# Attention with probabilities left unnormalised, and the reciprocal sums applied to the output

## The chip, the cores and the metric

The kernel runs on one core of one Trainium2 chip. The metric is device time in microseconds (us). The kernel before took 1541.53 us, the median of three runs (1538.05 to 1544.7). Its profiled execution took 1538.8 us, with a span of 1536.8 us from the first to the last instruction.

The core has five engines with a queue each: TensorE (PE; its weight loads are listed as PEld), VectorE (DVE), ScalarE (ACT), GpSimd (POOL) and SyncE (SP, which issues loads). TensorE writes PSUM only; VectorE and ScalarE read PSUM.

## The reference

One layer of a streaming encoder over 1024 frames of width 1024. Three token mixers run side by side on a normalised input, are gated and merged, and a feed-forward part follows. Two of the mixers are attention with 4 heads of 64: mixer A looks at a band of nine chunks of 64 frames with a relative bias, mixer B at the 256 keys that an indexer selects. Cut to what the change touches:

```
sc = q . k * d ** -0.5 + bias            # A: banded, B: masked to the selected keys
p  = softmax(sc)                         # exp(sc - max) / sum, over the keys
o  = p @ v                               # one 64-wide output per head and frame
...
merged = sigmoid(gt) * (y @ w_branch)    # summed over the three mixers
x = x + merged @ w_out
x = x + (silu(g) * u) @ w_ffn_out
```

Dividing the probabilities by their sum before the product with v, or the product by the sum after it, gives the same output.

## The kernel before, in words

Frames lie in 8 tiles of 128. All weights are split into a high and a low part (ScalarE copies, VectorE subtracts), and most products are three matmuls (`mm3`, L118 to L121) in that form. Streams of work are written as generators: A and B (attention), C (the recurrent mixer), G, F and W (gates), Z, Y (projections), K (top-k of the indexer, 32 counting rounds on VectorE and ScalarE), T. The string ORDER (L39) says which stream takes its next step. That is the order of the program. The order on each engine is then made by a planner that runs a timeline of its own (`schedule_with_timeline_sim=True`, L1461), so steps of neighbouring streams are interleaved, instruction by instruction. Each engine executes its queue in that order.

`attention` (L390) does one tile of 128 frames for two heads of mixer A or B. It is called for 8 tiles, two pairs of heads and two mixers: 32 calls, 64 heads. For each head, the scores go to PSUM (`dots`, L237). VectorE adds the mask or bias and takes the minimum of the negated scores into `nm` (L400). ScalarE takes the exponential of the row and its sum (L403). VectorE takes the reciprocal of the sum (L405) and multiplies the row with it (L406). TensorE transposes the row in blocks of 128 keys (L412) into banks of the pool tag T, which has two banks, and ScalarE copies them to SBUF as PT (L413). When both heads are done, the output `o` takes a bank of T too; per block of keys, one matmul for each head (L420) adds to its 64 rows of `o`, and ScalarE copies the result to `yT` (L422). A row has 128 to 640 keys in mixer A and 128 to 1024 in mixer B.

`sl` is a list of SBUF slots of 4 KB per partition; a tile takes the first free one and gives it back at the end of the list. `tbank` (L140) gives a PSUM bank of tag T. The T banks are also used by the turning of queries and keys (L352) and by some gate products.

Of the kernel before, what the change touches and what calls it, by code (L numbers as in the profile page):

```python
# [10 lines left out]
F32 = mybir.dt.float32  # L11
# [3 lines left out]
AF = mybir.ActivationFunctionType  # L15
OP = mybir.AluOpType
# [64 lines left out]
def hybrid_kernel(ctx: ExitStack, tc: tile.TileContext, x, small, cs, bias_a, lru_w, w_idx, w_zg, w_c, w_g, w_b,  # L81
                  w_o, w_fi, w_fo, out):
    nc = tc.nc
    V, S, G, PE = nc.vector, nc.scalar, nc.gpsimd, nc.tensor
    const = ctx.enter_context(tc.tile_pool(name="const", bufs=1))
    arena = ctx.enter_context(tc.tile_pool(name="arena", bufs=1))
    dram = ctx.enter_context(tc.tile_pool(name="dram", bufs=1, space=bass.MemoryType.DRAM))
    sl = Slots(arena, range(NRING, NSLOT))
    ring = Slots(arena, range(NRING))

    ident = const.tile([128, 128], F32, name="ident")
# [42 lines left out]
    def gbank(shape=(128, 512)):  # L134
        return psum.tile(list(shape), F32, name="G", tag="G", bufs=2)

    def sbank(shape=(128, 1024)):
        return psum.tile(list(shape), F32, name="S", tag="S", bufs=2)

    def tbank(shape=(128, 512)):  # L140
        return psum.tile(list(shape), F32, name="T", tag="T", bufs=2)
# [29 lines left out]
    for t0, tn in BATCH:  # L171
# [8 lines left out]
        w = 128 * tn  # L180
        for k in range(KD):
            if k % 2 == 0:
                sb = sbank()
            p = sb[:, 512 * (k % 2):512 * (k % 2) + w]
# [45 lines left out]
    def dots(sb, q, kh, kl, k0, w):  # L230
        o = 128 if w == 640 else 0
        segs = [(0, min(512 - o, max(w, 256)))]
        if w > 512 - o:
            segs.append((512 - o, w))
        for c0, c1 in segs:
            PE.matmul(sb[:, o + c0:o + c1], lhsT=q, rhs=kh[:, k0 + c0:k0 + c1], start=True, stop=False)
            PE.matmul(sb[:, o + c0:o + c1], lhsT=q, rhs=kl[:, k0 + c0:k0 + c1], start=False, stop=True)  # L237
        return sb[:, o:o + w]
# [4 lines left out]
    for g in range(2):  # L243
        zq = sl.get((128, 4, 4, 64), F32, "zq")
        zk = sl.get((128, 4, 2, 64), F32, "zk")
        for j in range(4):
            t = 4 * g + j
            p = gbank((128, 324))
# [49 lines left out]
    for i in range(2, NT):  # L298
        w = (i + 1) * 128
# [90 lines left out]
    def attention(i, b0, pr, qk, v, mask, yT, isB=False):  # L390
        nb = i + 1 - b0
        w = nb * 128
        q, kh, kl = qk
        PT = []
        for e in range(2):
            h = 2 * pr + e
            sb = dots(sbank(), q[e][:, 128 * i:128 * i + 128], kh[e], kl[e], 128 * b0, w)
            P = sl.get((128, 1024), F32, "P")
            nm = const.tile([128, 1], F32, name="nm", bufs=4)
            V.tensor_tensor_reduce(P[:, 0:w], sb, mask(h), -1.0, 3.0e38, op0=OP.add,  # L400
                                   op1=OP.min, accum_out=nm)
            sm_ = const.tile([128, 1], F32, name="sum", bufs=4)
            S.activation(P[:, 0:w], P[:, 0:w], AF.Exp, bias=nm, scale=-1.0, accum_out=sm_)  # L403
            rc = const.tile([128, 1], F32, name="rc", bufs=4)
            V.reciprocal(rc, sm_)  # L405
            V.tensor_scalar(P[:, 0:w], P[:, 0:w], rc, None, op0=OP.mult)  # L406
            pt_s = sl.get((128, 8, 128), F32, "PT")
            for c0 in range(0, nb, 4):
                c1 = min(c0 + 4, nb)
                pt = tbank((128, 4, 128))  # L410
                for b in range(c0, c1):
                    PE.transpose(pt[:, b - c0], P[:, 128 * b:128 * b + 128], ident)  # L412
                S.activation(pt_s[:, c0:c1], pt[:, 0:c1 - c0], AF.Copy)  # L413
            sl.free(P)
            PT.append(pt_s)
        o = tbank((128, 128))
        for b in range(nb):
            for e in range(2):
                h = 2 * pr + e
                PE.matmul(o[64 * e:64 * e + 64, :], lhsT=v[(b0 + b) // 4][:, (b0 + b) % 4, h, :],  # L420
                          rhs=PT[e][:, b, :], start=b == 0, stop=b == nb - 1, skip_group_check=True)
        S.activation(yT[:, 128 * i:128 * i + 128], o, AF.Copy)  # L422
        sl.free(*PT)

    def steps_A():
        for pr in range(2):
            bA = []
            for h in (2 * pr, 2 * pr + 1):
                bt = sl.get((128, 640), F32, "biasA")
                nc.gpsimd.dma_start(bt, bias_a[h])  # L430
                bA.append(bt)
            yA = sl.get((128, T), F32, "yA")
            qk = to_stack(zA[pr], ga8, smc("ga", 1))
            for i in range(NT):
                b0 = max(0, i - 4)
                w = (i + 1 - b0) * 128
                attention(i, b0, pr, qk, vA, lambda h: bA[h % 2][:, 640 - w:640], yA)
                if i == NT - 1:
                    sl.free(*bA)
                    nc.gpsimd.dma_start(y_dram[pr], yA)  # L440
                    sl.free(yA)
                    for a in qk:
                        sl.free(*a)
                    if pr == 1:
                        sl.free(*vA)
                yield
# [287 lines left out]
    def steps_B():  # L734
        for pr in range(2):
            yB = sl.get((128, T), F32, "yB")
            qk = to_stack(zB[pr], None, None)
            for i in range(NT):
                w = (i + 1) * 128
                mk = mask[i] if i >= 2 else m01[:, 256 - w:256]  # L740
                attention(i, 0, pr, qk, vB, lambda h: mk, yB, True)
                if i == NT - 1:
                    nc.gpsimd.dma_start(y_dram[2 + pr], yB)
                    sl.free(yB)
                    for a in qk:
                        sl.free(*a)
                    if pr == 1:
                        sl.free(*vB, *mp)
                yield
# [50 lines left out]
    def mbank():  # L800
        nb_[0] += 1
        return (gbank, tbank, sbank)[nb_[0] // 2 % 3]()[:, 0:512]
# [106 lines left out]
    yT = {}  # L909
# [34 lines left out]
    for ot in range(8):  # L944
# [13 lines left out]
        for q, (b, ks) in enumerate(((2, (4, 5, 6, 7)), (0, (0, 1)), (1, (2, 3)))):  # L958
            gt = load_gate(3 * ot + b) if ot else g0[b]
            mt = sl.get((128, T), F32, "mt") if q else None  # L960
            for hf in range(2):
                c = slice(512 * hf, 512 * hf + 512)
                m = M[ot // 2][hf][:, ot % 2]
                p = mbank()
# [107 lines left out]
    def bank(shape=(128, 512), at=0):  # L1072
        return psum.tile(list(shape), F32, name="B", tag=f"B{at}")

    for s_, n in enumerate(order):
# [5 lines left out]
        for t in range(4):  # L1081
            if n in "167":
                p = X[t]
            else:
                p = bank(at=4 + t)
# [379 lines left out]
```

## Time and profile before

| | before |
|---|---|
| median of three runs | 1541.53 us |
| profiled execution | 1538.8 us |
| its span | 1536.8 us |
| PE busy | 1479.5 us (96%) |
| PEld busy | 1237.1 us (80%) |
| DVE busy | 1119.4 us (73%) |
| ACT busy | 760.7 us (49%) |
| POOL busy | 108.4 us (7%) |
| mean granted TensorE clock | 0.991 |

The rows below are from the trace of the profiled execution. Times in timelines are microseconds from the start of the span. A group of instructions is given by line, engine, operation, output and inputs, shape and count, then after the bar its busy time in us and the mean duration of one in ns, then the idle time of its engine just before it and what ended that idle time. The granted clock is a share of TensorE's full 2.4 GHz. Matmuls overlap each other, so the time that one takes of the engine is read from start to start.

### The profile page before, as it was taken

The numbers are of one execution on the slowest core, as the hardware profiler recorded it, in microseconds if no ns is written. First come the engines' busy times: TensorE is split into PE (matmuls) and PEld (weight loads), VectorE is DVE, ScalarE is ACT, GpSimd is POOL, SyncE is SP. The second block draws the span as 40 slices with busy tenths as digits, with TensorE's granted clock in tenths as the row PEclk, the third lists the DMA queues.
The fourth block names the chain that finished last, engine by engine and source line by source line (L and its number), as shares of the span: only waits on it lengthen the run. The fifth ranks groups of instructions, "written<-read, shape, count | busy, mean of one in ns | idle before, by whom it ended". The sixth has DMA issues, their size and how long they took to land.

```text
span 1536.8 us, 19968 instructions
## 1 busy us (share of the span) xinstructions
PE 1479.5 (96%) x7612; PEld 1237.1 (80%) x7612; DVE 1119.4 (73%) x1949; ACT 760.7 (49%) x1188; POOL 108.4 (7%) x162
## 2 busy tenths in 40 slices
PE   6999889999999998999998989999999999999998
PEld 5898788989778886788886868888888888788887
DVE  4789999869666779767889786555555556478872
ACT  5566768774768656443214463333333333354340
POOL 1120011210000110010000210000000000000000
PEclk9999999999999999999999999999999999999999
DMA  4011202112112022357552322323232323697532
GB/s 175 28 45 42 96 18 97 56 69 83 41 42 69 29 96 70 117 178 300 213 182 79 110 96 96 110 96 110 96 110 96 110 96 123 231 364 267 189 126 89
DMA packets 51088, 178.40 MB, mean 116 GB/s; under 512 B 5872, under 2 KB 6000, under 8 KB 50992
## 3 DMA queue, kind: packets, MB, share of 16 engines
q1 hardware_dynamic: 36576, 128.36, 24.4%
q0 software_dynamic: 12688, 45.62, 7.6%
q10 hardware_dynamic: 1728, 3.15, 0.5%
q8 instruction: 60, 0.98, 0.3%
q14 instruction: 36, 0.29, 0.1%
HBM read 131.75 MB, written 45.35 MB: 115 GB/s over the span
## 4 chain that ended last, share of the span: by engine, by line
PE 63%; DVE 7%; ACT 3%; DMA 2%; issue 1%; SPq 0%; DVEq 0%; ACTq 0%
PE B L120 14%; PE B L121 14%; PE B L119 14%; PE G L121 4%; PE G L119 4%; PE G L120 4%; PE T L120 1%; PE T L119 1%; PE T L121 1%; PE S L119 1%; DMA fa<-pd 1%; PE S L121 1%; PE S L120 1%; PE T L420 1%; DVE ol L104 1%
## 5 line engine op out<-in xcount | busy, mean ns | idle before, releaser
L120 PE MATMUL B<-hl,fwh 128*128 128x512 f32 x528 | 205.5, 391 | 3.2 <-DVE hl L104 3.2
L119 PE MATMUL B<-hh,fwh 128*128 128x512 f32 x528 | 202.5, 391 | 3.3 <-ACT hh L103 3.3
L121 PE MATMUL B<-hh,fwl 128*128 128x512 f32 x528 | 198.3, 391 | 0.0
L119 PEld LDWEIGHTS B<-hh,fwh 128*128 128x128 f32 x528 | 99.5, 188 | 25.0 <-ACT hh L103 4.2
L120 PEld LDWEIGHTS B<-hl,fwh 128*128 128x128 f32 x528 | 99.5, 188 | 24.8 <-DVE hl L104 4.3
L121 PEld LDWEIGHTS B<-hh,fwl 128*128 128x128 f32 x528 | 99.6, 189 | 20.7
L120 PE MATMUL G<-wzl,hTh 128*128 128x256 f32 x384 | 110.9, 289 | 3.1 <-DVE wzl L104 3.1
L119 PE MATMUL G<-wzh,hTh 128*128 128x256 f32 x384 | 110.4, 290 | 1.3 <-ACT wzh L103 0.6
L121 PE MATMUL G<-wzh,hTl 128*128 128x256 f32 x384 | 110.9, 289 | 0.0
L104 DVE TENSOR_TENSOR fwl<-s,fwh 128x1024 fp32r<-128x1024 f32 x44 | 53.9, 1225 | 78.2 <-PE B L120 77.4
L120 PE MATMUL B<-fol,foh 128*128 128x512 f32 x264 | 102.8, 389 | 0.5 <-DVE fol L104 0.5
L119 PE MATMUL B<-foh,foh 128*128 128x512 f32 x264 | 101.4, 390 | 1.8 <-ACT foh L103 1.8
L121 PE MATMUL B<-foh,fol 128*128 128x512 f32 x264 | 101.7, 389 | 0.0
L649 ACT ACTIVATE junk_s<-score,ngS 128x1024 int8<-128x1024 f32 (+2 forms) x78 | 77.5, 993 | 17.3 <-DVE ngS L647 13.1
L121 PE MATMUL G<-hTh,wgl 128*128 128x512 f32 x192 | 76.5, 398 | 2.0 <-DVE wgl L104 2.0
L120 PEld LDWEIGHTS G<-wzl,hTh 128*128 128x128 f32 x384 | 74.5, 194 | 4.6 <-DVE wzl L104 3.7
L119 PE MATMUL G<-hTh,wgh 128*128 128x512 f32 x192 | 76.3, 397 | 1.1 <-ACT ge L544 1.1
L119 PEld LDWEIGHTS G<-wzh,hTh 128*128 128x128 f32 x384 | 74.6, 195 | 3.1 <-ACT wzh L103 1.1
L120 PE MATMUL G<-hTl,wgh 128*128 128x512 f32 x192 | 76.1, 396 | 0.0
L121 PEld LDWEIGHTS G<-wzh,hTl 128*128 128x128 f32 x384 | 74.7, 194 | 0.8 <-issue 0.5
L103 ACT ACTIVATE fw<-fb 128x512 fp32r<-128x512 f32 x22 | 13.9, 634 | 121.7 <-PE B L121 120.7
L103 ACT ACTIVATE foh<-fa 128x1024 fp32r<-128x1024 f32 x33 | 35.0, 1060 | 58.7 <-DMA fa<-pd 38.2
(488 smaller groups left out, 3863.6 us busy)
## 6 DMA issues: line engine op xcount, KB each, us to landing
fw<-in_w_fo SPq DMA_DIRECT2D x33, 512.0 KB, 5.4
fa<-pd SPq DMA_DIRECT2D x33, 512.0 KB, 5.1
gl<-gd SPq DMA_DIRECT2D x24, 512.0 KB, 6.0
fa<-in_w_fi SPq DMA_DIRECT2D x22, 512.0 KB, 3.6
fb<-in_w_fi SPq DMA_DIRECT2D x22, 512.0 KB, 3.5
pd<-act POOLq DMA_DIRECT2D x22, 512.0 KB, 5.3
ga<-in_w_g SPq DMA_DIRECT2D x18, 512.0 KB, 3.6
x<-in_x SPq DMA_DIRECT2D x12, 512.0 KB, 4.4
```

What stands on the lines that cost most here:

```text
L103: S.activation(hi, raw, AF.Copy)
L104: (eng or V).tensor_tensor(lo, raw, hi.bitcast(F32), op=OP.subtract)
L119: PE.matmul(o, lhsT=lh, rhs=rh, start=first, stop=False, **kw)
L120: PE.matmul(o, lhsT=lh, rhs=rl, start=False, stop=False, **kw)
L121: PE.matmul(o, lhsT=ll, rhs=rh, start=False, stop=last, **kw)
L420: PE.matmul(o[64 * e:64 * e + 64, :], lhsT=v[(b0 + b) // 4][:, (b0 + b) % 4, h, :], rhs=PT[e][:, b, :], start=b == 0, stop=b == nb - 1, sk ...
L649: S.activation(junk_s[:, 0:(i + 1) * 128], score[i], AF.Sign, bias=self.ng.bitcast(F32)[:, j:j + 1], accum_out=self.cnt[:, j:j + 1])
```

## The change

The probabilities stay as the exponential gives them. The two sums of a pair of heads go into the two columns of one tile. One reciprocal on VectorE writes each of them to 64 columns, 128 in all. TensorE transposes this 128x128 tile into the second half of the bank that holds the output, and ScalarE copies it to SBUF, into the first columns of the second head's P, which is for that reason given back only at the end of the call. The output matmuls follow. VectorE multiplies the output, read from PSUM, with that copy and writes `yT`, in place of ScalarE's copy. The slots of P of the second head and of both PT are given back in one call, in that order.

```diff
@@ attention
+        sums = const.tile([128, 2], F32, name="sum", bufs=4)
         for e in range(2):
...
-            sm_ = const.tile([128, 1], F32, name="sum", bufs=4)
-            S.activation(P[:, 0:w], P[:, 0:w], AF.Exp, bias=nm, scale=-1.0, accum_out=sm_)
-            rc = const.tile([128, 1], F32, name="rc", bufs=4)
-            V.reciprocal(rc, sm_)
-            V.tensor_scalar(P[:, 0:w], P[:, 0:w], rc, None, op0=OP.mult)
+            S.activation(P[:, 0:w], P[:, 0:w], AF.Exp, bias=nm, scale=-1.0, accum_out=sums[:, e:e + 1])
...
-            sl.free(P)
+            if e == 0:
+                sl.free(P)
             PT.append(pt_s)
-        o = tbank((128, 128))
+
+        rc = const.tile([128, 2, 64], F32, name="rc")
+        V.reciprocal(rc, sums[:, :, None].to_broadcast([128, 2, 64]))
+        on = tbank((128, 256))
+        o, n = on[:, 0:128], on[:, 128:256]
+        PE.transpose(n, rc.rearrange("p h d -> p (h d)"), ident)
+        ns = P[:, 0:128]
+        S.activation(ns, n, AF.Copy)
         for b in range(nb):
...
-        S.activation(yT[:, 128 * i:128 * i + 128], o, AF.Copy)
-        sl.free(*PT)
+        V.tensor_mul(yT[:, 128 * i:128 * i + 128], o, ns)
+        sl.free(P, *PT)
```

## Rows read from the trace of the kernel before

**Rows 1.** The page, part 1: busy us, share of the span, instructions.

```profile
PE 1479.5 (96%) x7612; PEld 1237.1 (80%) x7612; DVE 1119.4 (73%) x1949; ACT 760.7 (49%) x1188; POOL 108.4 (7%) x162
```

**Rows 2.** Stretches: length, PE, PEld, DVE, ACT, POOL busy (count), clock, DMA share, GB/s.

```profile
150.00:175.00 25.00, 21.50 (x109) 16.18 (x107) 24.75 (x91) 18.43 (x39) 0.55 (x1) 1.00 0.19 62
175.00:200.00 25.00, 20.17 (x115) 16.62 (x114) 24.71 (x83) 20.08 (x39) 1.07 (x2) 0.93 0.23 85
200.00:225.00 25.00, 24.20 (x210) 22.70 (x210) 23.27 (x76) 16.25 (x35) 3.73 (x4) 0.93 0.06 15
...
295.00:330.00 35.00, 35.00 (x233) 30.73 (x232) 26.34 (x62) 26.70 (x56) 5.28 (x4) 1.00 0.18 61
...
590.00:610.00 20.00, 17.04 (x164) 13.46 (x165) 19.89 (x29) 13.79 (x29) 0.53 (x1) 1.00 0.15 43
```

**Rows 3.** Waits of PE, 120 to 610 us: who for whom, total us, times, longest.

```profile
PE G L120 <- DVE wzl L104: 3.1, 1, 3.1
PE T L412 <- ACT yA L422: 2.7, 2, 1.7
...
PE T L412 <- ACT PT L413: 1.8, 3, 1.0
...
PE T L420 <- ACT PT L413: 1.1, 4, 0.5
PE T L412 <- DVE P L406: 0.6, 1, 0.6
```

**Rows 4.** Groups of DVE instructions: the multiplication by shapes, and the smallest masked add.

```profile
L406 DVE TENSOR_SCALAR P<-P,rc 128x640 f32<-128x640 f32 (+7 forms) x64 | 31.0, 491 | 0.6
...
L406 DVE TENSOR_SCALAR P<-P,rc 128x640 f32<-128x640 f32 x20 | 11.0, 550 | 0.2
...
L406 DVE TENSOR_SCALAR P<-P,rc 128x512 f32<-128x512 f32 x8 | 3.8, 483 | 0.1
L406 DVE TENSOR_SCALAR P<-P,rc 128x384 f32<-128x384 f32 x8 | 3.3, 414 | 0.1
...
L406 DVE TENSOR_SCALAR P<-P,rc 128x256 f32<-128x256 f32 x8 | 2.7, 349 | 0.1
...
L406 DVE TENSOR_SCALAR P<-P,rc 128x128 f32<-128x128 f32 x8 | 2.2, 290 | 0.1
...
L400 DVE CUSTOM_DVE_ANT_0 P<-S,biasA 128x128 f32<-128x128 f32 x4 | 1.1, 290 | 0.1
```

**Rows 5.** Views of single lines: ns min/median/max, first and last start in us.

```profile
L405 DVE RECIPROCAL rc<-sum x64: 136/157/165, 135.8 to 593.9; 128x1 f32<-128x1 f32 x64
...
L469 DVE RECIPROCAL sp_w<-sp_w x1: 173/173/173, 119.8 to 119.8; 128x4 f32<-128x4 f32 x1
...
L413 ACT ACTIVATE PT<-T x96: 253/490/616, 145.0 to 605.7; 128x512 f32<-128x512 f32 x44, 128x128 f32<-128x128 f32 x28, 128x256 f32<-128x256 f32 x12, 128x384 f32<-128x384 f32 x12
...
L422 ACT ACTIVATE yB<-T x16: 257/277/280, 406.3 to 607.6; 128x128 f32<-128x128 f32 x16
```

**Rows 6.** PE timeline at 208.5 us: start us, us, engine, line, operation.

```profile
208.49 0.28 PE L119 MATMUL G<-wzh,hTh 128*128 128x256 f32 x1
208.61 0.27 PE L412 MATMUL T<-ident,P 128*128 128x128 f32 x1
208.64 0.36 PE L120 MATMUL G<-wzl,hTh 128*128 128x256 f32 x1
208.84 0.28 PE L121 MATMUL G<-wzh,hTl 128*128 128x256 f32 x1
```

**Rows 7.** DVE timeline in the tail, 589 to 602 us.

```profile
590.64 0.16 DVE L405 RECIPROCAL rc<-sum 128x1 f32<-128x1 f32 x1
...
591.45 0.75 DVE L406 TENSOR_SCALAR P<-P,rc 128x1024 f32<-128x1024 f32 x1
...
593.92 0.15 DVE L405 RECIPROCAL rc<-sum 128x1 f32<-128x1 f32 x1
...
598.20 0.75 DVE L406 TENSOR_SCALAR P<-P,rc 128x1024 f32<-128x1024 f32 x1
```

## The prediction

> **What bounds the kernel now.** I read the page's engine shares first. TensorE is busy for 1479.5 of 1536.8 us, VectorE for 1119.4 [rows 1], so over the whole run TensorE sets the time and only its 57 us of idle time can be won. The change touches nothing before the first reciprocal at 135.8 us and nothing after the last output copy at 607.6 us [rows 5]; outside of that window the work stays as it is. So I then read the busy time by stretches inside it, looking for stretches where TensorE is not full, and who is full instead. Between 150 and 225 us VectorE is busy for 24.75 of 25, 24.71 of 25 and 23.27 of 25 us, while TensorE has 3.5, 4.8 and 0.8 us of idle time, and its granted clock in the last two of these stretches is 0.93, so it ran part of each at 1.2 instead of 2.4 GHz [rows 2]. There VectorE is the bound: it runs the top-k counting and the weight splits beside the first pair of local-attention heads. From 295 to 330 us it is the other way round, TensorE full and VectorE at 26.34 of 35 us. In the tail, 590 to 610 us, VectorE is again full (19.89 of 20) and TensorE has 3.0 us idle [rows 2]. The list of TensorE's waits over 120 to 610 us says what it waited for by name: 3.1 us for a weight split on VectorE (wzl), 2.7 us for the copy of an attention output out of PSUM (yA, two times in 32), 1.8 and 1.1 us for copies of transposed probabilities (PT), and only 0.6 us, once, for the multiplication that the change removes (P, L406) [rows 3].
>
> **The change part by part.** One head at one tile is a head-tile, of which there are 64; two heads at one tile make a pair-tile, of which there are 32.
>
> Removed on VectorE. Each head loses a one-column reciprocal of 157 ns [rows 5] and a multiplication of its probabilities. For the first pair of local heads, tiles 0 to 7, the widths are 128, 256, 384, 512 and four times 640: 290 + 349 + 414 + 483 + 4 x 550 = 3736 ns a head [rows 4]. Two heads: 7.5 us, and 16 x 0.157 = 2.5 us, so 10.0 us leave the stage in which VectorE is the bound.
>
> Added on VectorE, per pair-tile: a reciprocal written to 128 columns, and a product of 128x128 with one operand in PSUM. The product is like the smallest masked add, 128x128 out of PSUM, 290 ns [rows 4]. The wide reciprocal is not in the trace. Its rows are one column at 157 ns (136 at the least) and four columns at 173 ns [rows 5]: (173-157)/3 = 5.3 ns per column, so 157 + 127 x 5.3 = 0.83 us. Bounds: if it streamed like the multiplication it replaces, (550-290)/512 = 0.51 ns per column [rows 4], it is 0.22 us; from the fastest one-column reciprocal, (173-136)/3 = 12.3 ns per column, it is 1.70 us. I take 0.83, which comes from the medians. In the first stage that is 8 x (0.83+0.29) = 9.0 us, against 10.0 removed: -1.0 us, with ends 8 x 0.51 - 10.0 = -5.9 and 8 x 1.99 - 10.0 = +5.9. Because VectorE is the bound there, I count it in full. In the other three pairs of heads (24 pair-tiles) I count nothing: they run mostly where VectorE has slack, as in the 295 to 330 us stretch. If that cover were gone, the whole of it, 32 x 1.12 = 35.8 us added against 64 x 0.157 + 31.0 = 41.0 removed [rows 4, 5], would still be in the kernel's favour.
>
> The Trainium skill, "VectorE: DVE Perf Modes", section "First, the fixed hardware budget", says that the reciprocal is an iterative division with a repeat count of 8; with the 0.96 GHz of VectorE from the page "Trainium Kernel Development and Optimization" (NeuronCore Architecture), an estimate is 8.3 ns per column and 0.157 + 127 x 0.0083 = 1.21 us. The row's 5.3 ns per column lies below this and far above one cycle. By that rule the first stage would gain 8 x 1.50 - 10.0 = +2.0 us of VectorE work instead of losing 1.0.
>
> Added on TensorE: 32 transposes of 128x128. A single one among other matmuls stands in the trace, with starts at 208.49 (matmul), 208.61 (transpose), 208.64 and 208.84 (matmuls) [rows 6]. From 208.49 to 208.84 run two matmuls and the transpose, 0.35 us; a matmul alone takes 208.61 - 208.49 = 0.12, two 0.24. So 0.11 us each, 32 x 0.11 = +3.5 us. TensorE is the bound outside of the VectorE-bound stretches and the work comes on top, so this term is nearly sure; its low end is 0 for the 12 pair-tiles that lie in those stretches (8 in the first stage, 4 in the tail), 20 x 0.11 = 2.2.
>
> Added wait of the output matmuls. The transposed reciprocals n and the output o are halves of one tile in one PSUM bank; ScalarE copies n out before o may be written. On TensorE the 2 to 16 output matmuls are queued behind this, and all that follows in its order. The copy is as long as the old output copy, about 0.27 us [rows 5], and ScalarE's total is the same: one copy of 128x128 in, one out. Cover: the order of each engine is planned by a timeline, which puts other streams' matmuls in between. How well that works is seen on the 96 PT copies: 1.8 + 1.1 = 2.9 us of waits [rows 3, 5], 0.03 us each, so 32 x 0.03 = 1.0 us. In the last four pair-tiles there is hardly anything to put in between, and I count the copy as exposed: 4 x 0.27 = 1.1 us. Bounds: 0, and 32 x 0.27 = 8.6 us.
>
> For this wait the Trainium skill has a rule: "PSUM — Partial Sum Buffer", section "Terms", says that two engines at the same bank at once are an error, so the matmuls cannot slip under the copy; without the rule the 2.1 us of this term would be 0. No run shown so far tells which.
>
> Moved: the output leaves PSUM by a VectorE product instead of a ScalarE copy. That frees the bank for the next transposes, one of two banks that they all share. TensorE waited on this copy twice, 2.7 us [rows 3]. On VectorE the product stands in a fuller queue: a reciprocal and the multiplication that follows it with nothing else to wait for lie 0.81 us apart at 590.64 and 4.28 us apart at 593.92 [rows 7]. I add 0.8 us to each of those two waits, +1.6 us; ends 0 and 2 x 4.3 = 8.6.
>
> Removed wait: transposes follow the exponential directly, -0.6 us [rows 3]. What is late next is the copy PT, already in the sum. The second head's P stays allocated until the product; its two PT tiles were and are freed in the same call, so the order of the slots is unchanged and I cost it at nothing; if a later tile did need that slot early, it would wait one product, 0.29 us. No DMA is added or passed.
>
> Sum: 3.5 + 1.0 + 1.1 + 1.6 - 1.0 - 0.6 = +5.6 us. The profiled execution took 1538.8 us (span 1536.8 and 2.0 around it), which gives 1544.4. The median of the three runs, 1541.5, is 2.7 above the profiled one; the forecast for the median is 1547 us. By the reciprocal of the skill's page it would be 3.0 more, 1550.
>
> **Rivals.**
> *Faster: VectorE is relieved.* The reciprocal streams at 0.22 us, the first stage loses 5.9 us, TensorE's waits for splits there go, and with them the two stretches at 0.93 of the clock (2 x 25 x 0.07 = 3.5 us): -5.9 - 3.5 + 3.5 - 0.6 = -6.5, 1535. For it: 9.1 us of TensorE idle time at 150 to 225 us [rows 2]. Against it: the four-column reciprocal.
> *Slower: the reciprocal is the bill.* At 1.70 us the VectorE-bound stage grows by 5.9 instead of shrinking by 1.0: +12.5, 1554. This is also the case in which the change does not do what it says, take work off VectorE; it decides from about 0.96 us per reciprocal, where 8 x (0.96+0.29) = 10.0. For it: the two reciprocal rows; against it: they are single fast calls whose start-up may hide columns.
> *Slower: the bank is held.* If in the 12 pair-tiles where VectorE is full (8 in the first stage, 4 in the tail) each product keeps the bank 0.81 us longer and TensorE has nothing else to issue, 12 x 0.81 = 9.7 in place of 1.6: +13.7, 1555. For it: TensorE's longest attention wait is on just this release; against it: 30 of 32 releases cost nothing before. It decides when the waits on the output's release pass about 5 us.
> Besides, each engine's order is planned anew by the timeline, which can move some us either way; this widens all cases.
>
> **How the numbers follow.** Forecast 0.50, faster rival 0.15, reciprocal 0.18, bank 0.17. About 0.5% (7.7 us) is what a measurement of this kernel can tell from no change; from 1541.5 that is 1533.8 to 1549.2. The faster rival's own 1535 falls just short of it; with a favourable order of the rest it would pass, and so might a few of the forecast's cases: 0.14 faster. The two slower rivals nearly all lie above, and a tail of the forecast: 0.37 slower, 0.49 the same. The forecast's own range is 1541 to 1550; the range that leaves out two in ten is 1534 to 1558, from a little below the faster rival to a little above the slower ones.
>
> **What would show it.** In the profile after: 32 reciprocals of 128 columns near 0.83 us (0.22 or 1.70 would give a rival); no multiplication of P; VectorE busy some 5 us less (35.8 against 41.0); 32 more transposes, TensorE's instruction count up by 32; its waits on the ScalarE copy of n near 2 us, on the output's product near 4 us, on wzl in the 150 to 225 us stretch as before. ScalarE unchanged within 1 us. The prediction is wrong if the attention window ends earlier than before by several us, or if the time moves outside 128 to 610 us.

## The result, and the profile after

| | before | after |
|---|---|---|
| median | 1542.38 us (4 runs, 1538.05 to 1544.7) | 1560.68 us (4 runs, 1559.07 to 1561.78) |
| ratio of times | | 1.0128, 95% interval 1.0111 to 1.0145 |
| profiled execution, its span | 1538.8, 1536.8 us | 1561.78, 1560.0 us |
| TensorE idle in the span | 57.3 us | 76.1 us |
| mean granted TensorE clock | 0.991 | 0.984 |

The change made the kernel 18 us slower. The forecast was 5.6 us slower, 1547, with a range up to 1558; the time lies outside of it. Below, ratios of other kernels are to runs of the kernel before on the same chip; 0.001 is about 1.5 us.

The page's first part of the kernel after, against [rows 1]:

```profile
PE 1483.9 (95%) x7644; PEld 1243.6 (80%) x7644; DVE 1123.0 (72%) x1885; ACT 757.3 (49%) x1187; POOL 108.2 (7%) x162
```

TensorE has 32 instructions more, as planned, and is busy 4.4 us longer; 18.8 of the 23.2 us by which the span grew are idle time of TensorE. VectorE has 64 instructions less and is busy 3.6 us longer. So no engine got much more work: the engines wait more.

Not all of the 23.2 us belongs to the change. VectorE executes the same instructions in the same order in both kernels up to the first reciprocal, and this one starts at 140.3 us instead of 135.8 us [rows 5]. So this profiled execution was already 4.4 us late before anything that the change touches. The medians differ by 18.3 us.

Where the engines wait is read from the stretches of the kernel after (columns as in [rows 2]):

```profile
150.00:175.00 25.00, 22.78 (x106) 17.07 (x105) 24.51 (x80) 16.10 (x34) 0.55 (x1) 0.93 0.15 54
175.00:200.00 25.00, 20.65 (x130) 16.78 (x129) 24.50 (x82) 16.63 (x32) 1.06 (x2) 0.98 0.30 106
200.00:225.00 25.00, 23.96 (x193) 22.56 (x191) 24.36 (x75) 18.34 (x42) 1.10 (x3) 0.88 0.05 14
...
330.00:350.00 20.00, 14.72 (x100) 13.21 (x99) 11.16 (x21) 16.25 (x33) 0.54 (x1) 0.83 0.16 54
...
380.00:440.00 60.00, 49.37 (x215) 38.22 (x214) 42.09 (x54) 39.13 (x63) 1.06 (x2) 0.89 0.15 54
...
610.00:640.00 30.00, 23.43 (x178) 17.79 (x177) 28.25 (x38) 14.05 (x26) 0.53 (x1) 0.89 0.10 30
```

Two stretches of the kernel before that [rows 2] does not have:

```profile
330.00:350.00 20.00, 18.39 (x135) 16.12 (x134) 9.85 (x36) 11.75 (x25) 1.07 (x2) 0.91 0.15 53
...
380.00:440.00 60.00, 57.02 (x261) 44.43 (x260) 37.13 (x54) 42.49 (x63) 1.07 (x2) 0.97 0.16 54
```

The first three stretches, in which VectorE was the bound before, look much as in [rows 2]. What grew are the stretches from 330 to 350, 380 to 440 and 610 to 640 us: TensorE is idle for 5.3, 10.6 and 6.6 us, and the granted clock is 0.83 to 0.89, that is, part of each ran at 1.2 GHz. In the kernel before, the first two of them had 1.6 and 3.0 us of idle time and a clock of 0.91 and 0.97, and its own tail, 590 to 610 us, 3.0 us. The same clock times do not hold quite the same work, since the kernel after runs late.

Little of attention runs in the longest of these idle times. Of the 10.6 us, 7.4 lie between 395 and 410 us, when mixer A is done and mixer B has begun its first call only (one reciprocal, no product). ScalarE is busy for 14.43 of these 15 us and VectorE for 12.75:

```profile
395.00:410.00 15.00, 7.60 (x30) 5.02 (x28) 12.75 (x18) 14.43 (x20) 0.00 (x0) 0.79 0.01 2
```

How far attention has come shows in the rows of the output's last step; first the copies of mixer A in the kernel before (those of B are in [rows 5]), then the reciprocals and the products of the kernel after (first and last start in us):

```profile
L422 ACT ACTIVATE yA<-T x16: 253/270/278, 152.2 to 348.8; 128x128 f32<-128x128 f32 x16
```

```profile
L416 DVE RECIPROCAL rc<-sum x32: 942/948/954, 140.3 to 625.6; 128x128 f32<-128x128 f32 x32
```

The rows of the product by its line:

```profile
L427 DVE TENSOR_TENSOR yA<-T,P x16: 280/286/293, 163.1 to 363.2; 128x128 f32<-128x128 f32 x16
L427 DVE TENSOR_TENSOR yB<-T,P x16: 232/290/292, 422.0 to 638.4; 128x128 f32<-128x128 f32 x16
```

Mixer A ends at 363.2 instead of 348.8, +14.4 us; the first output of B comes 15.7 us late (422.0 against 406.3 in [rows 5]), the last 30.8 us late (638.4 against 607.6). Of these, 4.4 us are the late start. At its first output mixer A is 10.9 us late (163.1 against 152.2), at the end of its first pair of heads 10.1 us (246.4 against 236.3). So the first stage lost 5.7 us beyond the late start, all of it ahead of its first output, and 15.1 us more are lost between the first and the last output of mixer B, where the prediction counted next to nothing. Behind mixer B 7.6 us are won back.

VectorE's waits from 120 to 640 us in the kernel after (who for whom, total us, times, longest):

```profile
DVE yB L427 <- PE T L425: 12.6, 6, 4.0
...
DVE rc L416 <- PE T L419: 3.8, 7, 1.5
...
DVE yA L427 <- PE T L425: 3.1, 4, 1.6
```

TensorE's waits in the same stretch, against [rows 3]:

```profile
PE G L119 <- ACT wzh L103: 5.3, 1, 5.3
PE T L409 <- ACT PT L410: 4.5, 7, 2.0
...
PE T L409 <- DVE yB L427: 3.1, 2, 2.1
...
PE T L409 <- DVE yA L427: 2.6, 2, 2.2
...
PE T L425 <- ACT P L421: 2.1, 3, 1.0
```

VectorE stands for 15.7 us with the product at the head of its queue until TensorE has done the output matmuls, and for 3.8 us with a reciprocal until TensorE has read the one before from the tile that all calls share. TensorE in turn waits for the product (5.7 us), and for the copy of n (2.1 us).

Waiting at the head of a queue for the output matmuls is not new. In the kernel before ScalarE did it, for 23.6 us from 120 to 610 us, with its copy of the output:

```profile
ACT yB L422 <- PE T L420: 11.9, 9, 3.2
ACT yA L422 <- PE T L420: 11.7, 5, 3.5
```

The longest single wait of TensorE, 5.3 us for the weights wzh, does not come from VectorE's queue either. ScalarE makes wzh at 344.38 us; it had stood 2.77 us for a load of other weights, and two exponentials and a counting round stood ahead of wzh too:

```profile
340.98 1.06 ACT L103 ACTIVATE wcxh<-wcxr 128x1024 fp32r<-128x1024 f32 x1 [2.77 <-DMA wcxr<-in_w_c]
```

One round of this, in the tail. TensorE, then VectorE, kernel after:

```profile
611.02 1.31 PE L425 MATMUL T<-PT,v 128*64 128x128 f32 x20 [0.64 <-ACT P L421]
612.26 0.44 PE L409 MATMUL T<-ident,P 128*128 128x128 f32 x2
614.76 1.01 PE L409 MATMUL T<-ident,P 128*128 128x128 f32 x6 [2.06 <-DVE yB L427]
```

```profile
612.49 0.69 DVE L865 TENSOR_TENSOR s<-ga 128x512 f32<-128x512 f32 x1 [1.61 <-DMA ga<-in_w_g]
613.21 0.69 DVE L866 TENSOR_TENSOR s<-s,ga 128x512 f32<-128x512 f32 x1
613.82 0.68 DVE L789 TENSOR_TENSOR tq<-hTh,hTl 128x512 f32<-128x512 f32 x1
614.42 0.28 DVE L427 TENSOR_TENSOR yB<-T,P 128x128 f32<-128x128 f32 x1
```

The output matmuls end at 612.33. The product that empties their bank starts at 614.42, because an addition ahead of it in VectorE's queue waits 1.61 us for a load of weights and two more instructions follow. The next transposes need that bank and stand 2.06 us. Nothing in attention is late here; what is ahead of the product on its engine is.

The first call shows the same. From the reciprocal to the end of the product pass 23.1 us, of which the five steps themselves take 2.3 (the output matmuls 0.56). The rest is their places in the queues: between transpose and copy, for example, ScalarE does counting rounds of the indexer, a gate and a weight copy.

```profile
140.28 0.95 DVE L416 RECIPROCAL rc<-sum 128x128 f32<-128x128 f32 x1
...
150.15 0.27 PE L419 MATMUL T<-ident,rc 128*128 128x128 f32 x1
...
156.98 0.26 ACT L421 ACTIVATE P<-T 128x128 f32<-128x128 f32 x1
...
163.08 0.28 DVE L427 TENSOR_TENSOR yA<-T,P 128x128 f32<-128x128 f32 x1
```

How much of the span hangs on the length of the reciprocal, with the order as it is, can be read from the chain of work that ended last. It is followed back from the last instruction, at each step to what released it or to the instruction ahead of it on its engine. Of the 32 reciprocals two are on it, with 1.8 us (start and length in us):

```profile
588.45 0.95 DVE rc L416
...
618.91 0.86 DVE rc L416
```

By this chain a shorter reciprocal, with the same order on each engine and all other lengths as they are, would take less than 1.8 us off the span. What released an instruction is inferred from the trace, so this is an estimate.

### The profile page after: what moved, and what is told of

It is laid out like the page before. It is cut to its first block, busy times and chain, and to the rows that moved or that the text cites. A ratio compares the mean times of both kernels' runs of the same rounds, so it can differ in the third digit from the quotient of the medians.

```text
span 1560.0 us, 19966 instructions
## 1 busy us (share of the span) xinstructions
PE 1483.9 (95%) x7644; PEld 1243.6 (80%) x7644; DVE 1123.0 (72%) x1885; ACT 757.3 (49%) x1187; POOL 108.2 (7%) x162
## 4 chain that ended last, share of the span: by engine, by line
PE 62%; DVE 6%; ACT 3%; issue 2%; DMA 2%; POOL 0%; SPq 0%; DVEq 0%; POOLq 0%; ACTq 0%
PE B L120 14%; PE B L121 14%; PE B L119 14%; PE G L119 4%; PE G L120 3%; PE G L121 3%; PE T L121 1%; PE T L120 1%; PE T L119 1%; PE S L119 1%; PE S L121 1%; PE S L120 1%; PE T L425 1%; DMA fa<-pd 1%; DVE ol L104 1%
## 5 line engine op out<-in xcount | busy, mean ns | idle before, releaser
L121 PE MATMUL B<-hh,fwl 128*128 128x512 f32 x528 | 198.0, 390 | 0.0
L121 PEld LDWEIGHTS B<-hh,fwl 128*128 128x128 f32 x528 | 99.5, 188 | 20.7
L121 PE MATMUL G<-wzh,hTl 128*128 128x256 f32 x384 | 111.4, 291 | 0.0
L121 PE MATMUL B<-foh,fol 128*128 128x512 f32 x264 | 101.7, 389 | 0.0
L121 PE MATMUL G<-hTh,wgl 128*128 128x512 f32 x192 | 77.2, 402 | 0.5 <-DVE wgl L104 0.5
L121 PEld LDWEIGHTS G<-wzh,hTl 128*128 128x128 f32 x384 | 75.1, 196 | 1.0 <-issue 0.7
```

The costliest lines, as they stand in the source:

```text
L121: PE.matmul(o, lhsT=ll, rhs=rh, start=False, stop=last, **kw)
```

## The experiments

**The two new steps, each alone and both.** Three theories were put up. Theory 1: the product on VectorE, which waits for TensorE and holds the bank. Theory 2: the path of n (reciprocal, transpose, copy). Theory 3: the newly planned order of all engines, whatever the parts.

`n_act`: the path of n, with the ScalarE copy of the output.

```diff
-        V.tensor_mul(yT[:, 128 * i:128 * i + 128], o, ns)
+        S.activation(yT[:, 128 * i:128 * i + 128], o, AF.Copy)
```

> The changed kernel with its last step undone: the output leaves PSUM by the ScalarE copy again, so the product with the transposed reciprocals is left out (the output stays unnormalised). Reciprocal, transpose and copy of n stay. Theory 1 (the product on VectorE is the cost: VectorE stands in its queue until the output matmuls are done, and the bank waits for VectorE): most of the +18 us goes, 1542 to 1549. Theory 2 (the path of n is the cost: the wide reciprocal of 0.95 us, 32 transposes, and output matmuls behind the copy): still 1553 or more. Theory 3 (the newly planned order alone costs it, whatever the parts): no relation, anything from 1535 to 1560.

Measured: 1541.8 us, ratio 1.0015 (1.0002 to 1.0027).

`none_dve`: no path of n, the output leaves by VectorE.

```diff
-        rc = const.tile([128, 2, 64], F32, name="rc")
-        V.reciprocal(rc, sums[:, :, None].to_broadcast([128, 2, 64]))
-        on = tbank((128, 256))
-        o, n = on[:, 0:128], on[:, 128:256]
-        PE.transpose(n, rc.rearrange("p h d -> p (h d)"), ident)
-        ns = P[:, 0:128]
-        S.activation(ns, n, AF.Copy)
+        o = tbank((128, 128))
...
-        V.tensor_mul(yT[:, 128 * i:128 * i + 128], o, ns)
+        V.tensor_copy(yT[:, 128 * i:128 * i + 128], o)
```

> The changed kernel without the path of n: no reciprocal, no transpose, no copy of n; the output leaves PSUM by a VectorE copy of the same shape in place of the product (the output stays unnormalised). Theory 1: still slow, 1550 or more, although VectorE has 30 us less of reciprocals. Theory 2: as before or faster, 1530 to 1543. Theory 3: no relation.

Measured: 1531.4 us, 0.9957 (0.9941 to 0.9972).

`none_act`: no path of n (the first part of that diff), and the ScalarE copy.

> The changed kernel without the path of n and with the ScalarE copy of the output: normalisation is left out altogether, 41 us of VectorE work less than before and nothing added. Theories 1 and 2: faster than before, 1528 to 1538, since VectorE is the bound between 150 and 225 us. Theory 3: it may come out slower than before although it does strictly less.

Measured: 1530.9 us, 0.9949 (0.9933 to 0.9965).

`before_dveout`: the kernel before, its L422 as a VectorE copy.

```diff
-        S.activation(yT[:, 128 * i:128 * i + 128], o, AF.Copy)
+        V.tensor_copy(yT[:, 128 * i:128 * i + 128], o)
```

> The kernel before with one step of the change alone: the output leaves PSUM by a VectorE copy instead of the ScalarE copy; probabilities normalised as before. Theory 1: slower by 8 us or more, 1550 and up. Theory 2: within 5 us of before, 1538 to 1548. Theory 3: no relation.

Measured: 1535.0 us, 0.9973 (0.9961 to 0.9984), slightly faster than before.

Against the kernel without either step (0.9949), the VectorE output alone costs 0.0008, about 1 us; the path of n alone costs 0.0066, about 10 us; both together, the change, 0.0179, about 28 us. So theory 1 and theory 2 both fall as they were put. VectorE waits for the output matmuls in `none_dve` too, and it does no harm:

```profile
DVE yB L421 <- PE T L419: 7.6, 3, 3.9
DVE yA L421 <- PE T L419: 4.5, 5, 1.9
```

It is the two together, reciprocal on VectorE, transpose on TensorE, copy on ScalarE, output on TensorE, product on VectorE again, that cost 16 us more than their sum. Each of these kernels is also planned anew, so its engines run in an order of their own.

**Where in this loop.** The next three change one link of it each; the fourth was meant to test the planned order.

`thin_rc`, and `thin_again` later on another chip: the reciprocal of two columns, then spread.

```diff
-        V.reciprocal(rc, sums[:, :, None].to_broadcast([128, 2, 64]))
+        r2 = const.tile([128, 2], F32, name="r2", bufs=4)
+        V.reciprocal(r2, sums)
+        V.tensor_copy(rc, r2[:, :, None].to_broadcast([128, 2, 64]))
```

> The changed kernel with a cheaper reciprocal: two columns only (as in the row of 157 to 173 ns), then a VectorE copy that spreads them over 128 columns, instead of the 128-column reciprocal that the changed kernel's trace shows at 948 ns. Some 0.5 us of VectorE time less per pair-tile, 16 us in all. Theory 1 (the two VectorE steps of the loop reciprocal, transpose, copy, output, product are too long in VectorE's queue): 1543 to 1550. Theory 2 (TensorE waits behind the copy of n, because n and o share a bank): no change, 1556 to 1562. Theory 3 (planned order alone): no relation.

Measured: 1533.0 us, 0.9954 (0.9939 to 0.9969); faster than the kernel before, and better than any of the theories expected.

`pool_mul`: ScalarE copies the output out, GpSimd multiplies.

```diff
-        V.tensor_mul(yT[:, 128 * i:128 * i + 128], o, ns)
+        S.activation(yT[:, 128 * i:128 * i + 128], o, AF.Copy)
+        G.tensor_mul(yT[:, 128 * i:128 * i + 128], yT[:, 128 * i:128 * i + 128], ns)
```

> The changed kernel with the product moved: ScalarE copies the output out of PSUM as before, and GpSimd multiplies it in SBUF with the transposed reciprocals. Full result, no VectorE instruction waits for the output. Theory 1: 1540 to 1546, like the run that left the product out (1541.8). Theory 2: 1550 or more. Theory 3: no relation.

Measured: 1548.7 us, 1.0054 (1.0033 to 1.0074), between the two. GpSimd's products took 577 ns in mixer A and 1032 ns in mixer B on average; the medians are 462 and 470 ns, and a few long ones, up to 6120 ns, make the difference.

`n_last`: transpose and copy of n behind the output matmuls.

```diff
-        PE.transpose(n, rc.rearrange("p h d -> p (h d)"), ident)
-        ns = P[:, 0:128]
-        S.activation(ns, n, AF.Copy)
         for b in range(nb):
...
+        PE.transpose(n, rc.rearrange("p h d -> p (h d)"), ident)
+        ns = P[:, 0:128]
+        S.activation(ns, n, AF.Copy)
         V.tensor_mul(yT[:, 128 * i:128 * i + 128], o, ns)
```

> The changed kernel with the transpose of the reciprocals and its copy put behind the output matmuls instead of ahead of them: TensorE never waits for the copy of n, only the product on VectorE does. All instructions are those of the changed kernel. Theory 2: most of the loss goes, 1543 to 1550. Theory 1: no change or worse, 1555 to 1570, since the product on VectorE now waits for the output, the transpose and the copy. Theory 3: no relation.

Measured: 1552.7 us, 1.0081 (1.0053 to 1.0109): some 7 us of the loss go, not most of it.

`hold`: the kernel before, the second head's slot held to the end.

```diff
-            sl.free(P)
+            if e == 0:
+                sl.free(P)
...
-        sl.free(*PT)
+        sl.free(P, *PT)
```

> The kernel before, in which only the second head's P is given back at the end of the call, as the change does it: no instruction added or removed, only the planned order differs. Theories 1 and 2: within 4 us of before. Theory 3 (an order planned anew moves the time by itself): a move of 5 us or more either way is possible; its size says how much of any other move here can be the order alone.

Measured: 1539.6 us, 0.9998 (0.9983 to 1.0013). But this run does not test theory 3. Compared instruction by instruction, the traces of `hold` and of the kernel before show the same order on all five engines: nothing moved, so nothing was planned otherwise. The same holds for the two runs of this kind that stand below. In every other comparison the order on the engines changes together with the edit, and no run changes the order alone.

**Length or planning.** The cheap reciprocal takes 161 ns and its spread 223 ns, 0.38 us where the wide one took 0.95. In the profile of the second run, `thin_again`, VectorE waits less for the output (6.6 us against 15.7), and mixer B ends when it did in the kernel before (607.8 against 607.6). The wait for the shared tile, which was also expected to be shorter, is as long as in the changed kernel (3.9 against 3.8). First the page's line of busy times:

```profile
PE 1470.2 (96%) x7644; PEld 1232.5 (81%) x7644; DVE 1104.6 (72%) x1917; ACT 759.2 (50%) x1188; POOL 108.5 (7%) x162
```

Its groups by line (busy, mean ns of one, idle time before them):

```profile
L418 DVE COPY rc<-r 128x128 f32<-128x128 f32 x32 | 7.1, 223 | 4.1 <-PE T L421 3.9
L417 DVE RECIPROCAL r<-sum 128x2 f32<-128x2 f32 x32 | 5.2, 161 | 2.7 <-ACT P L403 2.5
```

VectorE's waits in it:

```profile
DVE yA L429 <- PE T L427: 3.9, 3, 2.5
DVE rc L418 <- PE T L421: 3.9, 3, 1.7
...
DVE yB L429 <- PE T L427: 2.7, 3, 1.1
```

And the product's rows of mixer B:

```profile
L429 DVE TENSOR_TENSOR yB<-T,P x16: 271/283/292, 406.2 to 607.8; 128x128 f32<-128x128 f32 x16
```

Either the length itself matters, or the planner takes the wide reciprocal for shorter than it is, so that all queues come late. `thin_pad` makes the cheap one as long, with instructions of a plain kind:

```diff
-        V.tensor_copy(rc, r2[:, :, None].to_broadcast([128, 2, 64]))
+        for _ in range(4):
+            V.tensor_copy(rc, r2[:, :, None].to_broadcast([128, 2, 64]))
```

> The cheap reciprocal (160 ns for two columns and 227 ns for the spreading copy), but the copy is made four times over, so that the two together take about the 0.95 us that the 128-column reciprocal took. Same results. Theory 1a (VectorE time as such: 32 times 0.95 us in the queue, with transpose, copy and output behind it): as slow as the changed kernel, 1553 to 1563. Theory 1b (the planner puts a lower time on the wide reciprocal than the 948 ns it takes, and every queue planned after it is late): mostly as fast as with one copy, 1533 to 1545, as copies are planned at about what they take.

Measured: 1557.5 us, 1.0111 (1.0083 to 1.0140). Theory 1b falls: plain copies of the same length cost as much. Its page's line of busy times is near that of the changed kernel again:

```profile
PE 1482.8 (95%) x7644; PEld 1243.2 (80%) x7644; DVE 1120.3 (72%) x2013; ACT 761.4 (49%) x1189; POOL 105.8 (7%) x162
```

Its spread by line, four times as many, and then its products in mixer B, whose last ends 27 us later than in `thin_again`:

```profile
L421 DVE COPY rc<-r 128x128 f32<-128x128 f32 x32 | 7.1, 222 | 0.3
```

```profile
L432 DVE TENSOR_TENSOR yB<-T,P x16: 269/284/293, 422.6 to 634.6; 128x128 f32<-128x128 f32 x16
```

Its waits on VectorE, from 120 to 640 us, are not those of the changed kernel: 8.9 us for the output, and 1.4 us for the shared tile, less than in the fast `thin_again`:

```profile
DVE yB L432 <- PE T L430: 4.9, 4, 2.9
DVE yA L432 <- PE T L430: 4.0, 4, 1.7
DVE rc L418 <- PE T L424: 1.4, 3, 1.0
```

So a longer step at this place makes the kernel slower, of whatever kind it is. That its length does so by being waited for is not shown. The three extra copies take 3 x 7.1 = 21.3 us in all; if every one held up the whole kernel, and all else kept its order and its length, that would be the most they cost, and the two spans differ by 26.6 us. Of these, TensorE is busy 12.6 us longer (1482.8 against 1470.2) with the same 7644 instructions, at a granted clock of 0.986 against 0.994, and idle 14.0 us longer. And the orders differ: TensorE's two queues part at about 145 us.

`thin_again`:

> The cheap reciprocal with one copy once more, for its profile beside that of the padded one on the same chip. Both theories: 1530 to 1536; VectorE's waits for the output and for the transpose of the reciprocals shorter than the 15.6 and 3.8 us of the changed kernel, TensorE's granted clock at 0.991 or more.

Measured: 1532.0 us, 0.9938 (0.9917 to 0.9959); granted clock 0.994.

`rc_in_p`: the wide reciprocal, without the shared tile.

```diff
-            if e == 0:
-                sl.free(P)
+            if e == 0:
+                P0 = P
...
-        rc = const.tile([128, 2, 64], F32, name="rc")
+        rc = P0[:, 0:128].rearrange("p (h d) -> p h d", h=2)
...
-        PE.transpose(n, rc.rearrange("p h d -> p (h d)"), ident)
+        PE.transpose(n, P0[:, 0:128], ident)
...
-        sl.free(P, *PT)
+        sl.free(P0, P, *PT)
```

> The changed kernel with the wide reciprocal, written into the first head's P instead of the one small tile that all 32 calls share, so that a reciprocal never waits until TensorE has read the one before. If this wait (3.8 us on VectorE in the changed kernel's profile) is what holds the loop together: 1545 to 1555. If the length of the reciprocal is the cause: 1556 to 1563.

Measured: 1551.1 us, 1.0069 (1.0043 to 1.0096).

`thin_n_last`: both diffs, the cheap reciprocal and n behind the output.

> The cheap reciprocal together with the transpose and copy of n behind the output matmuls. With the wide reciprocal the same move won 8 us of the 18. If the wait of the output matmuls for the copy of n is a cost of its own: 1525 to 1531, faster than with the cheap reciprocal alone (1533). If it only mattered because the reciprocal came late: no change, 1530 to 1537.

Measured: 1545.9 us, 1.0025 (1.0009 to 1.0041), slower than with the cheap reciprocal alone, which neither side expected. I take it that the transpose and the copy, put between output and product, make the way from the one to the other longer; no run tests that by itself, and the order on the engines is another one too.

**Work or waiting.** VectorE is idle for a fifth of the attention window, so it was open why 0.56 us less of it per pair-tile is worth 27 us. Here the same VectorE time, 0.67 us per pair-tile, is put once into the loop and once beside it. The base is `thin_in_p`, `rc_in_p` with the cheap reciprocal.

> The cheap reciprocal (two columns and a spreading copy), spread into the first head's P, so that no call waits for the transpose of the call before. With the wide reciprocal this took 10 us off. If VectorE's waits on that tile cost as much here: 1523 to 1528. If they cost only where the reciprocal is long: 1529 to 1535.

Measured: 1543.4 us, 1.0029 (1.0012 to 1.0046). Neither of the two: slower than with the shared tile. More on it below.

`thin_in_p_pad`: the spread four times, as in `thin_pad`.

> The same with the spreading copy made four times over, all ahead of the transpose: 0.56 us more VectorE time per pair-tile, on the loop. Latency: 1545 or more. Throughput: the same, 1545 or more; the run beside it tells them apart.

Measured: 1553.7 us, 1.0089 (1.0059 to 1.0119).

`thin_in_p_off`: the three extra copies into a tile that nobody reads.

```diff
         V.tensor_copy(rc, r2[:, :, None].to_broadcast([128, 2, 64]))
+        for _ in range(3):
+            V.tensor_copy(off, r2[:, :, None].to_broadcast([128, 2, 64]))
```

> The same with three more spreading copies into a tile that nobody reads: as much VectorE time as in the padded one, but nothing waits for it. Throughput: as slow as the padded one, 1545 or more, within 4 us of it. Latency: within 5 us of its base, 1525 to 1538.

Measured: 1542.8 us, 1.0021 (1.0005 to 1.0036). The 96 copies ran, 21.5 us of them, and the kernel is no slower than its base, in an order that was planned with them:

```profile
L421 DVE COPY off<-r 128x128 f32<-128x128 f32 x96 | 21.5, 224 | 1.3
```

`thin_act`: the spread on ScalarE.

```diff
-        V.tensor_copy(rc, r2[:, :, None].to_broadcast([128, 2, 64]))
+        S.activation(rc, r2[:, :, None].to_broadcast([128, 2, 64]), AF.Copy)
```

> The cheap reciprocal with the spreading copy on ScalarE in place of VectorE (one shared tile as in the changed kernel): 7 us less on VectorE, 8 us more on ScalarE, which is half idle, and one more hand-over on the loop. Throughput: 1525 to 1531, faster than with the copy on VectorE (1532). Latency: 1533 to 1542.

Measured: 1556.7 us, 1.0119 (1.0087 to 1.0151). VectorE has less to do than in any other kernel with the loop, and the time is as bad as the changed kernel's: the copy takes 304 ns on ScalarE instead of 223, and it adds a hand-over and a place in one more queue. The 81 ns are 2.6 us in 32 calls, against 28 us by which the kernel is slower than `thin_again`, so the length of the copy is not what costs here. What the hand-over costs, and what the order does, no run separates: after the same matmul of L121, at 144.90 and 144.95 us, TensorE goes on differently, in `thin_again` (first row) and here (second):

```profile
145.12 0.39 PE L119 MATMUL G<-hTh,wgh 128*128 128x512 f32 x1
...
145.72 0.50 PE L236 MATMUL S<-kh,qs 128*128 128x512 f32 x1 [0.38 <-DVE nm L401]
```

The copy's own row:

```profile
L418 ACT ACTIVATE rc<-r 128x128 f32<-128x128 f32 x32 | 9.7, 304 | 2.1 <-DVE r L417 1.9
```

**The slot.** `rc_in_p` and `thin_in_p` also hold the first head's slot longer. These two hold it and change nothing else:

```diff
-            if e == 0:
-                sl.free(P)
+            if e == 0:
+                P0 = P
...
-        sl.free(P, *PT)
+        sl.free(P0, P, *PT)
```

> The kernel with the cheap reciprocal and one shared tile (1532), in which the first head's P is also given back only at the end of the call; nothing is written into it. If the slot that is held longer costs the 11 us: 1540 to 1546. If it was the wait for the transposes of that P: 1529 to 1536.

Measured: 1532.5 us, 0.9943 (0.9928 to 0.9957).

> The changed kernel, with the first head's P given back only at the end of the call as well; nothing else. If the shared tile's wait was worth 10 us: no change, 1557 to 1564. If holding the slot, through the order planned with it, was worth it: 1548 to 1555.

Measured: 1559.8 us, 1.0117 (1.0100 to 1.0134). The slot alone does nothing in either; the order on all engines stays as it was, too. What is left of `thin_in_p` is that the reciprocals are written elsewhere, and the order planned with that. There the spread waits for the transposes of the P that it overwrites, 7.6 us of VectorE standing still, in place of 3.9 us for the shared tile:

```profile
DVE P L418 <- PE T L409: 7.6, 5, 3.8
```

But the same wait is 6.7 us in `rc_in_p`, against 3.8 us for the shared tile in the changed kernel, and there the kernel with the longer wait is the faster one. So the sum of these waits does not tell which kernel is slower, and why the P costs 11 us with the cheap reciprocal and saves 9 with the wide one is not shown.

```profile
DVE P L416 <- PE T L409: 6.7, 6, 2.7
```

Three kernels have the cheap reciprocal and the same instructions, 7644 on TensorE and 1917 on VectorE: `thin_again`, `thin_in_p` and `thin_n_last`. They lie up to 0.0087, about 13 us, apart. So who waits for whom, and the order planned with it, can move the time by half of what is to be explained, with no step made longer.

## Why the prediction was wrong, point by point

- **The sizes of the single steps were near.** The 128-column reciprocal took 948 ns (0.83 taken). The trace disagrees with the estimate by the rule of the Trainium skill, "VectorE: DVE Perf Modes", "First, the fixed hardware budget" (1.21 us): (948 - 157)/127 = 6.2 ns per column lies between the two. The product took 286 to 290 ns (290). TensorE got 32 transposes and 4.4 us more busy time (3.5), which does not measure the transposes: `thin_again` has them as well and is busy for 1470.2 us, 9.3 less than the kernel before. The output matmuls waited 2.1 us for the copy of n (2.1). The rule of the Trainium skill, "PSUM — Partial Sum Buffer", "Terms", agrees with this, but no run lets them go ahead under the copy. TensorE's wait for the output's release became 5.7 + 0.7 us, the last part by transposes of n (4.3). VectorE's groups: 30.4 + 9.2 = 39.6 us added (35.8) for 41.0 removed; VectorE was expected to be busy some 5 us less and is busy 3.6 us longer.
- **The step that failed** is "In the other three pairs of heads (24 pair-tiles) I count nothing: they run mostly where VectorE has slack", together with "Because VectorE is the bound there, I count it in full". Both price the new VectorE steps by the time that they occupy VectorE. The runs show that the place of this time decides: beside the loop from the sums to the product it cost nothing (`thin_in_p_off`: three more copies per pair-tile, 21.5 us in all, 0.0008 less than its base), in the loop it did (`thin_in_p_pad` 0.0060 over the same base, about 9 us; `thin_pad` 0.0173 over `thin_again`, about 27 us). Of the kernels whose loop ends with VectorE's product, those with about 1 us of VectorE ahead of the transpose are 0.7 to 1.3% slower than before (the changed kernel, `n_last`, `rc_in_p`, `thin_pad`, `thin_in_p_pad`), those with 0.38 us between 0.6% faster and 0.3% slower (`thin_again`, `thin_n_last`, `thin_in_p`, `thin_in_p_off`). The sum had no term for this loop: VectorE (0.95), TensorE, ScalarE (0.27), TensorE, VectorE (0.29), with a place in an ordered queue at each hand-over.
- **The new order of the queues** was named, "which can move some us either way; this widens all cases", and put at nothing in the sum. No run here puts a figure on it, and it is the rival that stands: the chain of the changed kernel has 1.8 us of reciprocals on it, `thin_pad` loses more than its copies take, and `thin_act` ten times what its longer copy adds. So it is shown that a longer step in this loop makes these kernels slower; whether because the engines wait for it, or because the planner arranges all queues otherwise around it, is not.
- **What was queued behind a wait** I named for TensorE only. The product waits at the head of VectorE's queue as well, 15.7 us, with 3.8 us more for the shared tile. These waits do not measure the loss: ScalarE waited 23.6 us for the same matmuls in the kernel before, VectorE 12.1 us in the fast `none_dve`, and only 8.9 and 1.4 us in the slow `thin_pad`. In the three stretches in which TensorE's idle time grew, part of the time ran at 1.2 GHz, granted clock 0.83 to 0.89.
- **The rivals.** "VectorE is relieved" did not happen in the changed kernel; in `none_act`, which adds nothing, the relief is worth 0.0051, about 8 us. "The reciprocal is the bill" named the right instruction and the right sign; its point, 0.96 us, was just about reached, but its mechanism, more VectorE work in the first stage, gives nothing at 0.95 us: 8 x (0.95 + 0.29) = 9.9 us added for 10.0 removed. "The bank is held" was there, 5.7 us against the 5 us that I set, but the output by VectorE without the loop costs 1 us, so it is no cause by itself.
- **What it says of the window.** At its last output the first stage is 10.1 us late in the profiled run, 4.4 of them from before the change. The other 5.7 are near the bound of +5.9, but not by its mechanism: they are there at the first output already, and the stage, 84.1 us from its first to its last output in the kernel before, takes 83.3.

What stays open: how much of the loss is the length of the loop and how much the order that the planner makes around it; a run would have to keep the order and change the length. Why the same copies cost 27 us with the shared tile and 9 us without it is open too. The waits on the shared tile do not explain it, 3.9 us in `thin_again` and 1.4 us in `thin_pad`. The lower clock and the idle time can be told apart in size (12.6 and 14.0 us between `thin_pad` and `thin_again`), not as cause and effect.

The kernel with the cheap reciprocal is faster than both: 0.9954, 0.9938 and, with the slot held, 0.9943 of the kernel before.

## What to carry to other kernels

A step that goes through several in-order queues in turn is not priced by the busy time that it adds or saves; a profile in which that engine has slack says nothing against such a loss. Look at the whole path, from first to last hand-over, and at what stands ahead of each step on its engine. To tell the two apart, put the same work once on the path and once beside it. And where a planner orders the queues, compare the orders in the traces before the edit is called the cause: here three runs that were to test the order had left it as it was, and all others had changed it. And a broadcast belongs behind an expensive operation, not ahead of it: two columns and a copy took 0.38 us where 128 columns took 0.95.

## What the runs showed of the hardware

- A VectorE reciprocal of float32 took 157 ns for 1 column, 161 for 2, 173 for 4 and 948 for 128: (948 - 157)/127 = 6.2 ns for each further column. A VectorE copy with a broadcast input took 223 ns for 128 columns, a ScalarE one 304 ns.
- A product of 128x128 in SBUF took GpSimd 462 ns in mixer A and 470 ns in mixer B in the median; single ones took up to 1444 and 6120 ns.
